# A hybrid decoder step on one core: the recurrent stage's small products placed on all four quarters of the TensorE array, and a pair's transposes put ahead of its value products

## The chip, the core and the metric

The kernel runs on one NeuronCore of one Trainium2 chip. The metric is the device time of one execution in microseconds (us), the median of several runs. The kernel before takes 2002.41 us (three runs, 1999.7 to 2004.16).

## The reference, cut to what matters

One decoder layer on 256 prompt positions and 8 sampled tokens (264 columns in all), float32: a SwiGLU feed-forward block, a mixing block (sliding-window attention beside an RWKV-7 recurrence), an output projection, a second feed-forward block, a final norm. The change touches only the recurrence, 16 heads of width 64:

```
def step(S, inp):                       # S: state [value i, key j] of a head
    sa = einsum('bhij,bhj->bhi', S, -kk_t)
    S = S * exp(lw_t) + sa[..., None] * (kk_t * a_t) + v_t[..., None] * k_t
    return S, einsum('bhij,bhj->bhi', S, r_t)
S, ys = lax.scan(step, S0, xs)          # 256 prompt steps; 1 step for each of the 8 sampled tokens
```

## The kernel before, in words

**Large products.** Every weight matrix is streamed from HBM in chunks of four 128x128 blocks (SyncE's queue, tile `raw`), split by ScalarE into a rounded part `hi` and by VectorE (or GpSimd) into a rest `lo`, and multiplied by TensorE in three fp32r products per block with 264 moving columns. These products have an accumulator tile `acc` as output (three PSUM banks). Four `hi` and four `lo` buffers let the split run ahead.

**Small work beside it.** Generators (tasks) are advanced one step after each chunk of the input projection and the output projection (`tick`). Each step issues its instructions there, and the Tile scheduler then orders each engine's instructions by its own timing estimate; every engine runs its list strictly in that order. All small products of the tasks write tiles named `m`, which share five PSUM banks (`mp()`, NM = 5): a sixth tile has to wait until the readers of the first are through.

**The recurrence** is done in chunks of 64 positions. Eight pairs of heads (`prep`, one task per pair) build the factors of the chunks; four batches of two pairs (`chain`) then solve and carry the state. A pair holds its two heads on partitions 0 to 63 and 64 to 127 (`HALF[0]`, `HALF[1]`, index h). A product with 64 contraction rows and 64 output columns occupies one quarter of the 128x128 array: its rows are the partitions of its inputs, its columns the partitions of its output. Written as (row half, column half), the kernel before uses (0,0) for h = 0 and (1,1) for h = 1. The places, with the names that the profile shows as out<-moving,stationary or with the two inputs in the other order:

- `XD,ld` in `prep`: 16 products per pair, state of a sampled token (64x64, in `ld`) by two columns of `XD`, into `dps`; ScalarE copies one column out (L488), VectorE reads the other from PSUM.
- `kr,bk`: eight 64x128 products into two banks, masked into `gm` by VectorE; then two transposes (L510), eight `uv,gm` products into `gv` (copied by L520 into `KR[:, 2]`), and four transposes (L523) copied into `BT`.
- `TN,gm` and `TT,zs` in `chain`: two groups of 16 products of 32x32 per batch, each copied out by two ScalarE copies (L596, L605) that the next group reads.
- `kr,TT`: 16 products per batch, 64 rows, 64 columns, moving 128 columns (`KR[r, 0:3:2]`: both W and UV at once), copied out by L619, L620, L621.
- `BT,W` and `gm,W`: 12 + 12 products per batch; `uv,BT` and `gm,uv`: 16 + 16 with all 128 rows and 64 columns.
- The carry loop: three steps per batch, each four products `S,PT` (or `N,PT`) and four `kr,S` (or `kr,N`), the latter added into `pY`, which ends in the tile `y` (L674).

Float32 products appear in the trace as two records each (16 products are x32); the large fp32r products and the transposes as one.

Of the kernel before, what the change touches and what calls it, by code (L numbers as in the profile page):

```python
# [10 lines left out]
ALU = mybir.AluOpType  # L11
AX = mybir.AxisListType

P = 128
NP = 256
NB = 8
# [8 lines left out]
HALF = (slice(0, 64), slice(64, 128))  # L25
# [22 lines left out]
def body(tc, I, O):  # L48
    nc = tc.nc
    V, A, G, TE, SP = nc.vector, nc.scalar, nc.gpsimd, nc.tensor, nc.sync  # L50
# [6 lines left out]
    def tt(e, out, a, b, op):  # L57
        return e.tensor_tensor(out=out, in0=a, in1=b, op=op)  # L58
# [14 lines left out]
    def mm(out, lhsT, rhs, start=True, stop=True, **k):  # L73
        TE.matmul(out, lhsT, rhs, start=start, stop=stop, **k)  # L74
# [20 lines left out]
    with ExitStack() as ctx:  # L95
# [17 lines left out]
        def mp():  # L113
            return pp.tile([P, 512], F32, tag="m", bufs=NM, name=uid("m"))
# [243 lines left out]
        def mixing_body(mx, n2, n3, XD):  # L358
# [60 lines left out]
            def prep(p, bt, k, xrr, xk, xv):  # L419
# [21 lines left out]
                W, Wi = tmp((P, 4, 65)), tmp((P, 4, 64))  # L441
# [14 lines left out]
                BK, KR = ring((P, 4, 3, 64), "bk", 2), ring((P, 3, 4, 64), "kr", NKR)  # L456
# [31 lines left out]
                A.copy(XD[:, 0, p, :], dv[:, 0])  # L488
                tt(V, dq, bps[:, T:T + 2 * NB].rearrange("p (s b) -> p s b", s=2), XD[:, 0:4:3, p, :], ALU.mult)
                tt(V, dq[:, 0], dv[:, 1], dq[:, 0], ALU.subtract)  # L490
                tt(V, XD[:, 7, p, :], dq[:, 0], dq[:, 1], ALU.add)
                yield
                gps = [mp(), mp()]
                for c in range(4):
                    for h in range(2):
                        r = HALF[h]
                        mm(gps[h][:, c * P:(c + 1) * P], BK[r, c, h:h + 2, :], KR[r, 0:2, c, :])
                for h in range(2):
# [3 lines left out]
                    for blk in range(2):  # L502
                        x = blk * 32
# [7 lines left out]
                for e in range(2):  # L511
                    for h in range(2):
                        A.copy(KR[HALF[h], 0, e:4:2, :],
                               kp[HALF[e], :256].rearrange("p (c t) -> p c t", c=2)[:, :, HALF[h]])
# [5 lines left out]
                A.copy(KR[:, 2], gv[:, :256].rearrange("p (c t) -> p c t", c=4))  # L520
                bp = mp()
                for c in range(4):
                    TE.transpose(bp[:, c * P:(c + 1) * P], BK[:, c, 0:2, :], ident)  # L523
# [3 lines left out]
                for h in range(2):  # L527
                    A.copy(BT[HALF[h], :, HALF[1]], bp[HALF[1 - h], :, HALF[1]])
                bt.BT[k] = BT
                yield  # L530
                bt.left -= 1

# [10 lines left out]
            def chain(bt):  # L543
                n = bt.n
# [13 lines left out]
                TT = ring((P, n * 4, 64), "TT", NTT)  # L558
# [11 lines left out]
                for g in range(ng):  # L570
                    d = Y[g * nr:(g + 1) * nr].rearrange("p j t -> p (j t)")
# [13 lines left out]
                yield  # L585
                ps = mp()
                for k in range(n):
                    for c in range(4):
                        for h in range(2):
                            j = k * 4 + c  # L590
                            mm(ps[h * 64 + 32:h * 64 + 64, j * 32:j * 32 + 32],
                               bt.Gm[k][h][h * 64:h * 64 + 32, c, 32:64], TN[h * 64:h * 64 + 32, j, :])
                zs = ring((P, n * 4, 32), "zs", 1)
                for h in range(2):
                    r = slice(h * 64 + 32, h * 64 + 64)
                    A.copy(zs[r], ps[r, :n * P].rearrange("p (c t) -> p c t", t=32))  # L596
                yield
                ps = mp()
                for j in range(4 * n):
                    for h in range(2):  # L600
                        r = slice(h * 64 + 32, h * 64 + 64)
                        mm(ps[h * 64:h * 64 + 32, j * 32:j * 32 + 32], zs[r, j, :], TT[r, j, 32:64])
                for h in range(2):
                    r = slice(h * 64, h * 64 + 32)
                    A.copy(TT[r, :, 32:64], ps[r, :n * P].rearrange("p (c t) -> p c t", t=32))  # L605
# [5 lines left out]
                wus = [mp() for _ in range(n)]  # L611
                for k in range(n):
                    for c in range(4):
                        for h in range(2):
                            r = HALF[h]
                            mm(wus[k][r, c * P:c * P + P], TT[r, k * 4 + c, :], bt.KR[k][r, 0:3:2, c, :])
                for k in range(n):
                    v = wus[k].rearrange("p (c t) -> p c t", c=4)
                    A.copy(W[:, k], v[:, 1:4, 0:64])  # L619
                    V.tensor_copy(uv[HALF[0], :, k, HALF[0]], v[HALF[0], :, 64:128])  # L620
                    A.copy(uv[HALF[1], :, k, HALF[1]], v[HALF[1], :, 64:128])  # L621
                yield
                pbs = [mp() for _ in range(n)]
                for k in range(n):
                    for c in range(1, 4):
                        x = (c - 1) * P
# [3 lines left out]
                        for h in range(2):  # L630
                            r = HALF[h]
                            mm(pbs[k][r, x + 64:x + P], W[r, k, c - 1, :], bt.Gm[k][h][r, c, 64:128])
                for k in range(n):
                    v = pbs[k][:, :384].rearrange("p (c t) -> p c t", c=3)
                    A.copy(PT[:, k], v[:, :, 0:64])
                    tt(V, bt.KR[k][:, 1, 1:4, :], v[:, :, 64:128], bt.KR[k][:, 1, 1:4, :], ALU.add)
# [7 lines left out]
                for k in range(n):  # L644
                    for c in range(4):
                        x = (k * 4 + c) * 64
                        for h in range(2):
                            r = HALF[h]
                            mm(pY[r, x:x + 64], uv[:, c, k, r], bt.Gm[k][h][:, c, 64:128],
                               k + c == 0, c == 0, skip_group_check=True)  # L650
                tt(V, N, pN[:, :n * 256].rearrange("p (k c t) -> p k c t", k=n, c=4),
                   bc(wc[:, bt.p0:bt.p0 + n, :].unsqueeze(3), (P, n, 4, 64)), ALU.mult)
# [2 lines left out]
                for c in range(1, 4):  # L655
                    ps = mp()
                    for k in range(n):
                        for h in range(2):
                            r = HALF[h]
                            mm(ps[r, k * 64:k * 64 + 64], PT[r, k, c - 1, :], S[r, k])  # L660
                    for k in range(n):
                        for h in range(2):
                            r = HALF[h]
                            x = (k * 4 + c) * 64
                            mm(pY[r, x:x + 64], S[r, k], bt.KR[k][r, 1, c, :], False, True, skip_group_check=True)
                    Z, Sn = ring((P, n, 64), "Z", 2), ring((P, n, 64), "S", 3)
                    for k in range(n):
                        stt(Z[:, k], S[:, k], wc[:, bt.p0 + k, c:c + 1], N[:, k, c, :], ALU.mult, ALU.add)
                    for k in range(n):
                        stt(Sn[:, k], ps[:, k * 64:k * 64 + 64], wc[:, bt.p0 + k, c:c + 1], Z[:, k], ALU.mult, ALU.add)  # L670
                    S = Sn
                    yield
                for k in range(n):
                    A.copy(Ys[k][:, :NP], pY[:, k * NP:(k + 1) * NP])  # L674
# [397 lines left out]
```

## Time and profile before

| | |
|---|---|
| median of the runs | 2002.41 us (1999.7 to 2004.16) |
| profiled execution | 2002.93 us, span in the trace 2001.1 us |
| granted TensorE clock, mean | 0.997 |
| busy: PE, DVE, ACT | 1980.3, 1304.9, 1055.0 us |
| HBM read | 347.59 MB, 179 GB/s over the span |
| stage of the recurrence and the attention | about 770 to 1160 us of the span |

The page gives each engine's busy time, the chain of work that ended last, and the costliest groups. The timeline gives instructions in order of time, like ones merged: start, time until the last of them ended, engine, line, operation, output<-inputs, shape (rows*columns of the array for PE, then moving rows x columns), and their number. PE rows overlap, since a product's stated time includes its run through the array; how long a group holds the engine is the distance from its start to the start of the next row.

### The profile page before, as it was taken

The page shows a single profiled execution, that of the slowest core. Times are in us where ns is not written, and L with a number is a line of the kernel's source. Part 1 is how long each engine was busy: PE and PEld are TensorE (multiplying, and loading weights), DVE is VectorE, ACT ScalarE, POOL GpSimd, SP SyncE. Part 2 cuts the span into 40 slices and gives each one's busy share as a digit, 9 for nine tenths or more (in the row PEclk, how much of TensorE's full clock was granted, in tenths as well). Part 3 has the DMA queues.
Part 4 walks back from the last instruction along what each step waited for, and adds up shares of the span by engine and source line. Part 5 has one row for each costly group of instructions (what it writes and reads, how often), then busy time and mean ns, then how long its engine had stood idle before and what let it go on. Part 6 is the DMA issues. An engine that isn't in the chain of part 4 may idle for free.

```text
span 2001.1 us, 45661 instructions
## 1 busy us (share of the span) xinstructions
PE 1980.3 (99%) x17116; PEld 1945.5 (97%) x17116; DVE 1304.9 (65%) x2550; ACT 1055.0 (53%) x2089; POOL 340.3 (17%) x437
## 2 busy tenths in 40 slices
PE   9999999999999999999999999999999999999998
PEld 9999999999999999998988899999999999999997
DVE  5865555655556577688768766765666666666665
ACT  5644444444444456765555655654444444444445
POOL 0401001010010122121123553120101001010012
PEclk9999999999999999999999999999999999999999
DMA  7666666665666567554555546565666666666664
GB/s 231 177 193 192 184 193 191 184 184 177 186 176 185 182 197 221 158 149 130 152 143 148 155 141 195 175 182 177 189 188 193 182 188 195 184 192 183 195 180 145
DMA packets 229230, 358.74 MB, mean 179 GB/s; under 512 B 42616, under 2 KB 84240, under 8 KB 229008
## 3 DMA queue, kind: packets, MB, share of 16 engines
q1 hardware_dynamic: 223120, 349.72, 58.4%
q10 hardware_dynamic: 5888, 6.11, 1.0%
q8 instruction: 134, 2.20, 0.5%
q14 instruction: 88, 0.72, 0.1%
HBM read 347.59 MB, written 10.22 MB: 179 GB/s over the span
## 4 chain that ended last, share of the span: by engine, by line
PE 94%; DVE 3%; DMA 2%; SPq 1%; ACT 0%; issue 0%; POOL 0%; DVEq 0%; POOLq 0%; ACTq 0%
PE acc L74 86%; PE m L74 7%; DVE lo L58 0%; DVE Xt L58 0%; DMA Xt<-sa 0%; DMA raw<-in_gu 0%; DVE st L58 0%; DMA xg<-in_xT 0%; SPq L126 0%; DVE y L58 0%; PE m L523 0%; DVE t L703 0%; ACT hi L127 0%; DMA TT<-sb 0%; SPq L555 0%
## 5 line engine op out<-in xcount | busy, mean ns | idle before, releaser
L127 ACT CAST hi<-raw 128x512 fp32r<-128x512 f32 (+2 forms) x1304 | 779.0, 602 | 822.0 <-PE acc L74 733.5
L58 DVE TENSOR_TENSOR lo<-raw,hi 128x512 fp32r<-128x512 f32 (+1 forms) x1248 | 854.0, 688 | 540.0 <-ACT hi L127 515.5
L74 PE MATMUL acc<-s,hi 128*128 128x264 f32 x5940 | 1109.7, 286 | 0.3 <-ACT hi L127 0.2
L74 PEld LDWEIGHTS acc<-s,hi 128*128 128x128 f32 x5940 | 923.8, 188 | 7.4 <-issue 2.2
L74 PE MATMUL acc<-s,lo 128*128 128x264 f32 x2970 | 848.9, 286 | 2.5 <-DVE lo L58 2.5
L74 PEld LDWEIGHTS acc<-s,lo 128*128 128x128 f32 x2970 | 558.7, 188 | 7.0 <-DVE lo L58 3.6
L74 PE MATMUL acc<-t,hi 128*128 128x264 f32 x2752 | 502.8, 284 | 0.0
L74 PEld LDWEIGHTS acc<-t,hi 128*128 128x128 f32 x2752 | 425.9, 188 | 0.0
L74 PE MATMUL acc<-t,lo 128*128 128x264 f32 x1376 | 388.5, 284 | 0.0
L58 POOL TENSOR_TENSOR t<-t,t 128x264 f32<-128x264 f32 (+1 forms) x148 | 150.8, 1019 | 1149.0 <-ACT hi L127 789.6
L74 PEld LDWEIGHTS acc<-t,lo 128*128 128x128 f32 x1376 | 258.2, 188 | 0.1
L74 PE MATMUL acc<-y,hi 128*128 128x264 f32 x648 | 123.9, 284 | 0.0
L74 PEld LDWEIGHTS acc<-y,hi 128*128 128x128 f32 x648 | 101.2, 188 | 0.2
L74 PE MATMUL acc<-y,lo 128*128 128x264 f32 x324 | 91.2, 282 | 0.0
L58 DVE TENSOR_TENSOR t<-acc,t 128x264 f32<-128x264 f32 x156 | 67.4, 432 | 36.3 <-PE acc L74 36.1
L58 POOL TENSOR_TENSOR lo<-raw,hi 128x512 fp32r<-128x512 f32 x56 | 74.5, 1333 | 58.3 <-ACT hi L127 34.0
L58 POOL TENSOR_TENSOR o<-o,o 128x264 f32<-128x264 f32 x43 | 35.9, 834 | 187.3 <-ACT o L68 183.4
L74 PE MATMUL acc<-o,hi 128*128 128x264 f32 x324 | 62.4, 282 | 0.0
L74 PEld LDWEIGHTS acc<-y,lo 128*128 128x128 f32 x324 | 60.9, 188 | 0.0
L61 DVE SCALAR_TENSOR_TENSOR s<-acc,s 128x264 f32<-128x264 f32 x96 | 40.5, 427 | 16.0 <-PE acc L74 15.5
L74 PEld LDWEIGHTS acc<-o,hi 128*128 128x128 f32 x324 | 49.9, 188 | 0.0
L74 PE MATMUL m<-s,hi 128*128 128x264 f32 x260 | 48.1, 285 | 0.0
(249 smaller groups left out, 1350.5 us busy)
## 6 DMA issues: line engine op xcount, KB each, us to landing
raw<-in_gu SPq DMA_DIRECT2D x688, 256.0 KB, 3.4
raw<-in_dn SPq DMA_DIRECT2D x224, 256.0 KB, 2.9
raw<-in_win SPq DMA_DIRECT2D x152, 256.0 KB, 3.5
raw<-in_dn SPq DMA_DIRECT2D x160, 192.0 KB, 2.7
raw<-in_wout SPq DMA_DIRECT2D x48, 256.0 KB, 3.3
raw<-in_wout SPq DMA_DIRECT2D x32, 128.0 KB, 3.1
s<-xsp SPq DMA_DIRECT2D x16, 132.0 KB, 3.7
ld<-in_sT SPq DMA_DIRECT2D x16, 128.0 KB, 3.8
```

What stands on the lines that cost most here:

```text
L58: return e.tensor_tensor(out=out, in0=a, in1=b, op=op)
L61: return V.scalar_tensor_tensor(out=out, in0=a, scalar=s, in1=b, op0=op0, op1=op1)
L74: TE.matmul(out, lhsT, rhs, start=start, stop=stop, **k)
L127: A.copy(hi[:, :w], raw[:, :w])
```

## The change

Products that stood on the two diagonal quarters are now spread over four. Where two products of one half h follow each other, every other one gets the opposite column half, `HALF[1 - h]`, so that its result stands on the wrong partitions, in a bank of its own; the copy out of PSUM reads it there and writes it to the right partitions. Such a copy handles one half at a time, so one copy of 128 partitions becomes one of 128 partitions with half the columns and two of 64 partitions. `dps` and `gv` take two banks in place of one. The 32x32 products get a second column position for the batch's second pair, and their loops run over c outside k; each group's two copies become four. The 16 products `kr,TT` with 128 moving columns become 28 products with 64 (W is not computed for the first chunk). In a pair, the four transposes into `bp` and the copies into `BT` now come before the `uv,gm` products. In the carry loop the two kinds of product alternate pair by pair. `sub(h, x)` is the 32 partitions from 64h + 32x. The diff, without the renaming of slices:

```diff
-                dps = mp()
+                dps = [mp(), mp()]
                 for i in range(NB):
                     for h in range(2):
                         r = HALF[h]
-                        mm(dps[r, 2 * i:2 * i + 2], st[i // 4][r, i % 4, :], XD[r, 6:8, p, i])
-                dv = dps[:, 0:16].rearrange("p (b s) -> p s b", s=2)
-                A.copy(XD[:, 0, p, :], dv[:, 0])
+                        x = i // 2 * 2
+                        mm(dps[i % 2][HALF[h ^ i % 2], x:x + 2], st[i // 4][r, i % 4, :], XD[r, 6:8, p, i])
+                dv = [d[:, 0:NB].rearrange("p (b s) -> p s b", s=2) for d in dps]
+                A.copy(XD[:, 0:7:6, p, 0:NB:2], dv[0])
+                for h in range(2):
+                    A.copy(XD[HALF[h], 0:7:6, p, 1:NB:2], dv[1][HALF[1 - h]])
...
-                tt(V, dq[:, 0], dv[:, 1], dq[:, 0], ALU.subtract)
+                tt(V, dq[:, 0], XD[:, 6, p, :], dq[:, 0], ALU.subtract)
...
-                gv = mp()
-                for c in range(4):
-                    for h in range(2):
-                        r, o = HALF[h], HALF[1 - h]
-                        mm(gv[r, c * 64:c * 64 + 64], bt.Gm[k][h][o, c, 0:64], bt.UV[o, c, k, r])
-                A.copy(KR[:, 2], gv[:, :256].rearrange("p (c t) -> p c t", c=4))
                 bp = mp()
...
                 bt.BT[k] = BT
+                gv = [mp(), mp()]
+                for c in range(4):
+                    for h in range(2):
+                        r, o = HALF[h], HALF[1 - h]
+                        x = c // 2 * 64
+                        mm(gv[c % 2][HALF[h ^ c % 2], x:x + 64], bt.Gm[k][h][o, c, 0:64], bt.UV[o, c, k, r])
...
-                for k in range(n):
-                    for c in range(4):
+                for c in range(4):
+                    for k in range(n):
                         for h in range(2):
                             j = k * 4 + c
-                            mm(ps[h * 64 + 32:h * 64 + 64, j * 32:j * 32 + 32],
-                               bt.Gm[k][h][h * 64:h * 64 + 32, c, 32:64], TN[h * 64:h * 64 + 32, j, :])
+                            mm(ps[sub(h, 1 - k), j * 32:j * 32 + 32],
+                               bt.Gm[k][h][sub(h, 0), c, 32:64], TN[sub(h, 0), j, :])
...
+                        for ps, a, m in (pW, 0, 0), (pU, 2, 1):
+                            for h in range(2):
+                                if a or c:
+                                    mm(ps[HALF[h ^ m], j * 64:j * 64 + 64], TT[HALF[h], j, :],
+                                       bt.KR[k][HALF[h], a, c, :])
...
-                            mm(pbs[k][r, x:x + 64], W[r, k, c - 1, :], bt.BT[k][r, c, r])
-                        for h in range(2):
-                            r = HALF[h]
-                            mm(pbs[k][r, x + 64:x + P], W[r, k, c - 1, :], bt.Gm[k][h][r, c, 64:128])
+                            mm(pP[HALF[1 - h], x:x + 64], W[r, k, c - 1, :], bt.BT[k][r, c, r])
+                        for h in range(2):
+                            r = HALF[h]
+                            mm(pG[r, x:x + 64], W[r, k, c - 1, :], bt.Gm[k][h][r, c, 64:128])
...
-                            mm(pY[r, x:x + 64], S[r, k], bt.KR[k][r, 1, c, :], False, True, skip_group_check=True)
+                            mm(pY[HALF[1 - h], x:x + 64], S[r, k], bt.KR[k][r, 1, c, :], False, True,
+                               skip_group_check=True)
...
-                    A.copy(Ys[k][:, :NP], pY[:, k * NP:(k + 1) * NP])
+                    for h in range(2):
+                        A.copy(Ys[k][HALF[h], :NP], pY[HALF[1 - h], k * NP:(k + 1) * NP])
```

What TensorE's list holds at three places. First, the products `XD,ld` of the fifth pair and what follows them; before, with the bonus product `t,C` ahead and the first batch's `TN,gm` behind (the number after an `m` tells the PSUM tile):

```order
L74 MATMUL m_12799<-t_12681,C 128x280 [waits DVE_49,PE_49,Pool_49]
L74 MATMUL m_12802<-XD,ld_12725 64x2 [waits DMAHW5_49]
L74 MATMUL m_12802<-XD,ld_12725 64x2 x7
L74 MATMUL m_12802<-XD,ld_12727 64x2 [waits DMAHW7_49]
L74 MATMUL m_12802<-XD,ld_12727 64x2 x7
L74 MATMUL m_12848<-TN_12790,gm_11263 32x32 [waits PE_49]
```

and now:

```order
L74 MATMUL m_12823<-t_12705,C 128x280 [waits DVE_49,PE_49,Pool_49]
L74 MATMUL m_12826<-XD,ld_12749 64x2 [waits DMAHW5_49]
L74 MATMUL m_12826<-XD,ld_12749 64x2
L74 MATMUL m_12827<-XD,ld_12749 64x2 [waits PE_49]
L74 MATMUL m_12827<-XD,ld_12749 64x2
L74 MATMUL m_12826<-XD,ld_12749 64x2 x2
L74 MATMUL m_12827<-XD,ld_12749 64x2 x2
L74 MATMUL m_12826<-XD,ld_12751 64x2 [waits DMAHW7_49]
L74 MATMUL m_12826<-XD,ld_12751 64x2
L74 MATMUL m_12827<-XD,ld_12751 64x2 x2
L74 MATMUL m_12826<-XD,ld_12751 64x2 x2
L74 MATMUL m_12827<-XD,ld_12751 64x2 x2
```

The place in the list is the same; two tiles (12826 on the diagonal quarters, 12827 on the other two) alternate every two products.

Second, `kr,TT` of the first batch; before, 16 products with 128 moving columns:

```order
L74 MATMUL m_12958<-kr_11127,TT_11726 64x128 [waits DMAHW1_49,DVE_49,Activation_49]
L74 MATMUL m_12959<-kr_11492,TT_11726 64x128 [waits PE_49]
L74 MATMUL m_12958<-kr_11127,TT_11726 64x128 [waits DMAHW4_49,Activation_49]
L74 MATMUL m_12958<-kr_11127,TT_11726 64x128 x6
L74 MATMUL m_12959<-kr_11492,TT_11726 64x128 x7
```

and now 28 products with 64, the first half of which is:

```order
L74 MATMUL m_12990<-kr_11127,TT_11738 64x64 [waits DMAHW7_49,DVE_49,Activation_49]
L74 MATMUL m_12990<-kr_11127,TT_11738 64x64 [waits DMAHW1_49,Activation_49]
L74 MATMUL m_12989<-kr_11127,TT_11738 64x64 [waits PE_49]
L74 MATMUL m_12989<-kr_11127,TT_11738 64x64
L74 MATMUL m_12990<-kr_11127,TT_11738 64x64 x2
L74 MATMUL m_12989<-kr_11127,TT_11738 64x64 x2
L74 MATMUL m_12990<-kr_11127,TT_11738 64x64 x2
L74 MATMUL m_12989<-kr_11127,TT_11738 64x64 x2
L74 MATMUL m_12990<-kr_11127,TT_11738 64x64 x2
```

Each pair of heads now sends eight products to the off-diagonal quarters (12990) and six to the diagonal ones (12989).

Third, the end of ScalarE's work for the same links: the copies out of `XD,ld`, `TN,gm` and `TT,zs`; before:

```order
L488 COPY XD<-m_12802 128x8 [waits PE_49]
L596 COPY zs_12865<-m_12848 32x256 [waits PE_49]
L596 COPY zs_12865<-m_12848 32x256
L127 CAST hi_13258<-raw_13257 128x512 [waits DMAHW7_49,DVE_49,PE_49]
L68 ACTIVATE t_12828<-pj_10571,vec 128x256 [waits DVE_49]
L605 COPY TT_11726<-m_12906 32x8x32 [waits PE_49]
L605 COPY TT_11726<-m_12906 32x8x32
```

and now:

```order
L489 COPY XD<-m_12826 128x2x4 [waits PE_49,Pool_49]
L491 COPY XD<-m_12827 64x2x4 [waits PE_49]
L491 COPY XD<-m_12827 64x2x4
L610 COPY zs_12892<-m_12875 32x128 [waits PE_49]
L610 COPY zs_12892<-m_12875 32x128 x3
L127 CAST hi_13249<-raw_13248 128x512 [waits DMAHW6_49,PE_49,Activation_49]
L621 COPY TT_11738<-m_12935 32x4x32 [waits PE_49]
L621 COPY TT_11738<-m_12935 32x4x32 x3
```

Five copies became eleven; the split of the next weight chunk (`hi`) still stands between the two groups. Over the whole list ScalarE has 225 rows of copies where it had 193 (a row can stand for several), VectorE has 28 where it had 32. In two of the eight pairs (the sixth and the eighth) the list has runs of five to seven `XD,ld` products into one tile; in the fifth and the seventh the `uv,gm` products stand as four into one tile, eleven large products, and four into the other; and in the first two batches six `BT,W` products of the first pair stand ahead of its six `gm,W`.

More of the change, by code (lines that the diff above doesn't have):

```diff
@@ L529, in prep @@
                 bt.BT[k] = BT
+                gv = [mp(), mp()]
[4 more added lines that the diff above has]
+                        mm(gv[c % 2][HALF[h ^ c % 2], x:x + 64], bt.Gm[k][h][o, c, 0:64], bt.UV[o, c, k, r])
+                gv = [g[:, :P].rearrange("p (c t) -> p c t", c=2) for g in gv]
+                A.copy(KR[:, 2, 0:4:2], gv[0])
+                for h in range(2):
+                    A.copy(KR[HALF[h], 2, 1:4:2], gv[1][HALF[1 - h]])
                 yield
@@ L610, in chain @@
                 N = ring((P, n, 4, 64), "N", 1)
-                wus = [mp() for _ in range(n)]
+                pW, pU = mp(), mp()
                 for k in range(n):
                     for c in range(4):
+                        j = k * 4 + c
+                        for ps, a, m in (pW, 0, 0), (pU, 2, 1):
+                            for h in range(2):
+                                if a or c:
+                                    mm(ps[HALF[h ^ m], j * 64:j * 64 + 64], TT[HALF[h], j, :],
+                                       bt.KR[k][HALF[h], a, c, :])
@@ new lines, in chain @@
+                pW, pU = (ps.rearrange("p (k c t) -> p k c t", k=n, c=4) for ps in (pW, pU))
+                A.copy(W, pW[:, :, 1:4, :])
+                V.tensor_copy(uv[HALF[0], :, :, HALF[0]].rearrange("p c k t -> p k c t"), pU[HALF[1]])
+                A.copy(uv[HALF[1], :, :, HALF[1]].rearrange("p c k t -> p k c t"), pU[HALF[0]])
+                yield
+                pP, pG = mp(), mp()
+                for k in range(n):
+                    for c in range(1, 4):
+                        x = (k * 3 + c - 1) * 64
@@ L633, in chain @@
+                pP, pG = (ps[:, :n * 192].rearrange("p (k c t) -> p k c t", k=n, c=3) for ps in (pP, pG))
+                for h in range(2):
+                    A.copy(PT[HALF[h]], pP[HALF[1 - h]])
                 for k in range(n):
-                    v = pbs[k][:, :384].rearrange("p (c t) -> p c t", c=3)
-                    A.copy(PT[:, k], v[:, :, 0:64])
-                    tt(V, bt.KR[k][:, 1, 1:4, :], v[:, :, 64:128], bt.KR[k][:, 1, 1:4, :], ALU.add)
+                    tt(V, bt.KR[k][:, 1, 1:4, :], pG[:, k], bt.KR[k][:, 1, 1:4, :], ALU.add)
@@ L673, in chain @@
                 for k in range(n):
-                    A.copy(Ys[k][:, :NP], pY[:, k * NP:(k + 1) * NP])
+                    for h in range(2):
+                        A.copy(Ys[k][HALF[h], :NP], pY[HALF[1 - h], k * NP:(k + 1) * NP])
                     A.copy(Ys[k][:, NP:T], XD[:, 7, bt.p0 + k, :])
```

37 lines of the change are left out of this document (15 added, 22 removed).

## Prediction, made before the changed kernel was run

> **What bounds the kernel.** I read the page first: busy shares and the chain that ended last.
>
> ```profile
> span 2001.1 us, 45661 instructions
> PE 1980.3 (99%) x17116; PEld 1945.5 (97%) x17116; DVE 1304.9 (65%) x2550; ACT 1055.0 (53%) x2089; POOL 340.3 (17%) x437
> PE 94%; DVE 3%; DMA 2%; SPq 1%; ACT 0%; issue 0%; POOL 0%; DVEq 0%; POOLq 0%; ACTq 0%
> ```
>
> TensorE (PE) is on the path for 94% of the span. A busy PE can still be waiting inside, so I took stages next (us; busy time and count of PE, its weight loads PEld, DVE, ACT, POOL; clock; DMA share; GB/s) and then PE's waits (total us, times, longest).
>
> ```profile
> 100.00:690.00 590.00, 590.00 (x4856) 590.00 (x4855) 339.70 (x577) 277.49 (x486) 60.76 (x56) 1.00 0.62 186
> 900.00:1000.00 100.00, 95.87 (x1165) 88.96 (x1165) 81.75 (x237) 59.66 (x146) 17.52 (x41) 1.00 0.53 142
> 770.00:1160.00 390.00, 380.54 (x3984) 351.10 (x3984) 293.67 (x824) 252.24 (x625) 106.95 (x190) 1.00 0.54 152
> ...
> PE m L74 <- ACT t L68: 3.3, 2, 2.2
> PE acc L74 <- DVE lo L58: 2.5, 4, 0.8
> PE m L74 <- DVE N L58: 1.1, 1, 1.1
> ```
>
> From 100 to 690 us the large products come every 590/4856 = 0.1215 us, without a gap. In the recurrent stage, 770 to 1160, PE is idle for 390 − 380.5 = 9.5 us. So a us less of PE work there should be nearly a us less of time, as long as VectorE (75% busy there, 82% from 900 to 1000) and ScalarE (65%) keep up.
>
> **What the small products cost now.** Timeline around the fifth pair and the first batch (start, us, what):
>
> ```profile
> 910.88 1.10 PE L74 MATMUL m<-XD,ld 64*64 64x2 f32 x32
> 911.90 0.69 PE L74 MATMUL m<-TN,gm 32*32 32x32 f32 x32
> 912.52 1.16 PE L74 MATMUL m<-kr,bk 64*128 64x128 f32 x16
> ...
> 919.12 2.02 PE L74 MATMUL m<-kr,TT 64*64 64x128 f32 x32
> 921.07 0.44 PE L510 MATMUL m<-C,kr 128*128 128x128 f32 x2
> 921.44 0.68 PE L74 MATMUL m<-uv,gm 64*64 64x64 f32 x16
> 922.05 0.66 PE L523 MATMUL m<-C,bk 128*128 128x128 f32 x4
> ...
> 924.23 0.33 PE L74 MATMUL m<-BT,W 64*64 64x64 f32 x4
> 924.39 0.28 PE L74 MATMUL m<-gm,W 64*64 64x64 f32 x4
> ...
> 925.56 0.28 PE L74 MATMUL m<-gm,W 64*64 64x64 f32 x4
> 925.77 1.15 PE L74 MATMUL m<-uv,BT 128*64 128x64 f32 x32
> ...
> 933.44 0.45 PE L74 MATMUL m<-S,PT 64*64 64x64 f32 x8
> 933.72 0.40 PE L74 MATMUL m<-kr,S 64*64 64x64 f32 x8
> 934.05 0.39 PE L74 MATMUL acc<-s,lo 128*128 128x264 f32 x1
> ```
>
> From 924.39 to 925.56 there are ten such rows of four records: 1.17/40 = 29.2 ns a record with two quarters in use, so each quarter takes 58.5 ns a record. `XD,ld` moves only two columns and still takes 32 × 29.2 = 0.93 of its 1.02 us: the quarter's weight load sets that, not the columns. The rest, 0.09 to 0.14 us a group, is the turn from one array shape to the next and stays.
>
> **Do four quarters run at once?** No row before has that. The nearest (a short window each, then two whole groups):
>
> ```profile
> 912.52 0.38 PE L74 MATMUL m<-kr,bk 64*128 64x128 f32 x2
> ...
> 1095.86 0.32 PE L74 MATMUL m<-uv,bk 128*32 128x128 f32 x4
> ...
> 1096.83 0.28 PE L74 MATMUL m<-s,bk 128*32 128x1 f32 x16
> 1097.04 0.43 PE L74 MATMUL m<-t,s 128*64 128x256 f32 x1
> ```
>
> The first window (20 ns wide) holds the starts of both row halves, over the same columns into two banks. The second (25 ns) holds the starts of four column quarters that share all their rows. In the third, 16 records with their own weights fit in 0.21 us, 13 ns each with the turn included. So row halves overlap, column quarters overlap, and starts can follow each other within 14.6 ns. The bounds per record are 14.6 (four at once) and 29.2 ns (no gain); I take 14.6, since the rows of four column quarters are nearest.
>
> [...]
>
> **The sum, term by term** (two-at-once time halved, turns left alone):
> - `XD,ld`, eight pairs: 0.93 to 0.47 us, 8 × 0.47 = 3.7.
> - `uv,gm`, eight pairs: 16 × 29.2 = 0.47 of 0.61 us, halved, 8 × 0.23 = 1.9.
> - `TN,gm` and `TT,zs`: 0.62 us from the row to the next, 0.12 of it the turn; 8 groups × 0.25 = 2.0.
> - `kr,TT`: 1.95 us, 0.15 of it the turn. Now the fullest quarters take eight products, 16 records × 58.5 = 0.94 us; 4 × (1.80 − 0.94) = 3.4.
> - `BT,W` and `gm,W`: 48 records, 1.54 us with the turn; 4 × 0.70 = 2.8.
> - carry loop: 16 records a step, 12 steps × 0.23 = 2.8.
>
> That makes 16.6 us. `uv,BT`, `gm,uv` and `kr,bk` keep their shape: nothing. From it go the places where the list of the changed kernel doesn't alternate: two pairs of `XD,ld` (−0.8), two batches' first half of `BT,W` (−0.7), two pairs of `uv,gm` cut in two by large products (−0.5). The two lists hold 185 and 186 changes of array shape, so turns cost −0.1. Left: **14.5 us of PE time**. The transposes moved ahead of `uv,gm` are the same transposes between the same two turns: nothing.
>
> **The copies.** ScalarE durations (min/median/max ns):
>
> ```profile
> L488 ACT COPY XD<-m x8: 166/166/166, 811.0 to 1028.2; 128x8 f32<-128x8 f32 x8
> L520 ACT COPY kr<-m x8: 372/373/375, 816.1 to 1037.1; 128x256 f32<-128x256 f32 x8
> L596 ACT COPY zs<-m x8: 363/364/367, 912.6 to 1124.9; 32x256 f32<-32x256 f32 x8
> L513 ACT COPY kr<-m x32: 254/260/265, 813.8 to 1034.1; 64x128 f32<-64x128 f32 x32
> L674 ACT COPY y<-m x8: 349/369/379, 937.3 to 1147.8; 128x256 f32<-128x256 f32 x8
> ```
>
> A copy costs by its columns, hardly by its partitions: 0.17 us for 8, 0.26 for 128, 0.37 for 256. `XD`: two more, +0.33, eight times 2.7. `gv`: three of 0.26 for one of 0.37, 8 × 0.41 = 3.3. `zs` and `TT`: four of 0.26 for two of 0.36, 8 × 0.31 = 2.5. `y`: two more of 0.37 in four batches, 3.0. `W`, UV and `PT` trade fewer copies for wider ones, about even. Together +11.5 us of ScalarE, which is idle for 390 − 252 = 138 us of the stage: hidden as work. As latency, `zs` and `TT` stand right ahead of products that read them; between `TN,gm` and `TT,zs` the list has `kr,bk` (912.52 to 913.62, 1.1 us) and six large products (0.7 us), which cover four copies (1.04 us) unless a 0.6 us split of a chunk goes first. If the cover is gone, 0.31 us × 8 = 2.5. I charge these in full, and 1.0 more for PE's waits on `lo`, since PE reaches its large products 0.25 to 0.7 us earlier after each burst while VectorE does not: the four waits of 2.5 us in all would grow by 0.25 each. Give-back 3.5, between nothing and all of 14.5.
>
> **Sum.** 2002.93 (profiled execution; span 2001.1) − 14.5 + 3.5 = 1991.9. The median of the runs is 0.5 below the profiled execution: **1991.4 us**.
>
> **Rivals.**
> - **VectorE takes over** between 900 and 1100 us: the 82% becomes 87% if 6 us leave that stretch, and its list runs in order, with the solve's small steps between the `lo`. Each of some 36 bursts (8 pairs with two each, 4 batches with five) then gives back 0.25 us: 9. 2002.4 − 14.5 + 9 = 1997. For it: VectorE's share there, and that `lo` is already waited for. Against: the rows above have PE waiting for VectorE for 2.5 and 1.1 us in all.
> - **The quarters take turns** (the change doesn't do what it says): 29.2 ns stays. `kr,TT` becomes 56 × 29.2 = 1.64 for 1.80, −0.6 over four batches; the copies' latency adds 1: 2003. Against: the column-quarter rows. [...]
> - **PSUM banks** (slower): `XD,ld` and `uv,gm` claim one more of the five `m` banks each, 16 claims. A claim can last until VectorE has read the bonus tile behind the copies:
>
> ```profile
> 912.02 0.17 ACT L488 COPY XD<-m 128x8 f32<-128x8 f32 x1 [1.70 <-PE m L74]
> ...
> 913.82 0.17 DVE L58 TENSOR_TENSOR t<-m,XD 128x16 f32<-128x16 f32 x1
> ```
>
>  `XD,ld` ended at 911.9 and that read at 914.0, 2.1 us later. If PE, which runs in order, sat out 1.4 us per claim with the large products queued behind it: 16 × 1.4 = 22, 2010 us. It cancels the gain at 14.5/16 = 0.9 us a claim and shows as slower from 1.2. For it: five banks are just what one pair needs from the bonus product to `kr,bk` (1 + 2 + 2), and `TN,gm` makes it six. Against: the list puts large products in where it expects such a wait, and PE's waits of today are for values (`t`, `lo`, `N`).
>
> **How the numbers follow.** Forecast 1991.4, own range 1986 to 1996: 0.60. More than that (waits of today gone too): 0.04. VectorE: 0.14, three quarters of it still faster by over 0.2%. Turns: 0.09, of it 0.07 no change, the rest on both sides. Banks: 0.13. A difference under 0.2% (4 us) is about what a measurement of this kernel can't tell from no change. Faster 0.60 + 0.04 + 0.11 + 0.01 = 0.76; same 0.03 + 0.07 = 0.10; slower 0.13 + 0.01 = 0.14. The range takes in the forecast, VectorE and the turns: 1985 to 2004; the banks and the tail below are left out, under 0.2.
>
> **What would show it.** `XD,ld` x32 from its start to the next row about 0.55 us (1.02 now), `uv,gm` x16 0.38, `TN,gm` 0.37, `kr,TT` x56 1.1, `BT,W` with `gm,W` 0.85: then four run at once. If these distances stay, it was turns. If they shrink and the span doesn't, PE's waits tell which rival: on `lo` (VectorE), on `zs` or `TT` (copies), or idle time ahead of `kr,bk`, `uv,gm` with ScalarE or VectorE as releaser (banks). The forecast is wrong if small products shrink by under 10 us or PE's idle time in the stage grows by over 8.

## The result, and the profile after

**No change that can be measured.** The changed kernel takes 2003.59 us (median of 14 runs, 2001.57 to 2005.91), the kernel before 2001.71 beside it (14 runs, 1999.70 to 2006.54): ratio 1.0006, 95% interval 0.9998 to 1.0014 (all ratios here are of the means, so they differ a little from those of the medians). 1991.4 was predicted, 12 us less. The execution profiled after is the fastest of its 14 (2001.57), that of before (2002.93) lies 1.2 above its median; so the two profiles differ by -1.4 us where the medians differ by +1.9. What follows compares the profiles and says so.

The page after: span, busy engines, the shares of the chain of work that ended last; then the stages (columns as before), of which the middle row is the recurrent stage.

```profile
span 1999.8 us, 45897 instructions
PE 1969.5 (98%) x17212; PEld 1933.6 (97%) x17212; DVE 1301.4 (65%) x2546; ACT 1065.4 (53%) x2137; POOL 343.1 (17%) x437
PE 91%; DVE 4%; DMA 2%; ACT 1%; issue 1%; SPq 1%; POOL 0%; ACTq 0%; DVEq 0%; POOLq 0%
```

```profile
100.00:690.00 590.00, 590.00 (x4856) 590.00 (x4855) 340.14 (x577) 277.28 (x486) 60.52 (x56) 1.00 0.61 186
770.00:1160.00 390.00, 372.06 (x4093) 341.19 (x4093) 290.65 (x820) 264.43 (x676) 109.73 (x193) 0.99 0.53 152
900.00:1000.00 100.00, 91.49 (x1202) 83.95 (x1203) 80.52 (x231) 61.30 (x159) 17.97 (x43) 0.97 0.50 138
```

PE is busy 10.8 us less (1980.3 to 1969.5), so the work did shrink. But span minus busy, PE's idle time, went from 20.8 to 30.3 us, and PE's share of the chain from 94 to 91%. The timeline around the fifth pair and the first batch shows the smaller products:

```profile
910.79 0.64 PE L74 MATMUL m<-XD,ld 64*64 64x2 f32 x32
911.36 0.45 PE L74 MATMUL m<-TN,gm 32*32 32x32 f32 x32
911.75 1.49 PE L74 MATMUL m<-kr,bk 64*128 64x128 f32 x16
...
917.12 1.15 PE L74 MATMUL m<-kr,TT 64*64 64x64 f32 x56
918.20 0.44 PE L513 MATMUL m<-C,kr 128*128 128x128 f32 x2
...
919.01 0.45 PE L74 MATMUL m<-uv,gm 64*64 64x64 f32 x8
...
922.12 0.45 PE L74 MATMUL m<-uv,gm 64*64 64x64 f32 x8 [1.13 <-ACT W L637]
...
923.09 0.56 PE L74 MATMUL m<-BT,W 64*64 64x64 f32 x12
925.62 0.59 PE L74 MATMUL m<-gm,W 64*64 64x64 f32 x6 [1.97 <-ACT uv L639]
```

From its start to the next row `XD,ld` takes 0.57 us (1.02 before; 0.55 foretold), `TN,gm` 0.39 (0.62; 0.37), `kr,TT` 1.08 (1.95; 1.1). The starts of four records of `kr,TT` lie 6 to 7 ns apart, then in most of the group comes a step of 38: 58 ns for four, where two quarters took 58 for two. So four quarters do run at once. The two waits in the last rows are new. ScalarE's rows for the same time show where they come from:

```profile
921.05 0.51 ACT L68 ACTIVATE t<-pj,vec 128x256 f32<-128x256 f32 x1 [4.30 <-DVE pj L58]
921.59 0.48 ACT L637 COPY W<-m 128x384 f32<-128x384 f32 x1
...
924.99 0.58 ACT L639 COPY uv<-m 64x512 f32<-64x512 f32 x1 [1.18 <-DVE uv L638]
```

The last record of `kr,TT` ends at 918.3, but the copy of its result into `W` starts at 921.59: in ScalarE's list it stands behind an operation that waits 4.30 us for VectorE's `pj`. The copy itself takes 0.48 us. `uv,gm` starts when it is done (922.12 after 922.07), though it doesn't read `W`, so it waits for the bank that the copy empties. The copy into `uv` waits 1.18 us for VectorE's copy of the other half, which starts at 924.26, between two steps of the solve. PE's waits in the stage, after (total us, times, longest):

```profile
PE acc L74 <- DVE lo L58: 4.6, 4, 1.8
PE m L74 <- ACT W L637: 3.2, 2, 2.1
PE m L74 <- DVE st L58: 3.1, 2, 2.4
PE m L74 <- ACT t L68: 3.1, 3, 1.7
PE m L74 <- ACT uv L639: 2.2, 2, 2.0
```

Before, `lo` stood for 2.5 us, `W` for 0.3, `st` and `N` together for 1.3, `uv` for nothing; the two rows of before that the prediction doesn't show are:

```profile
PE m L74 <- ACT W L619: 0.3, 1, 0.3
PE m L74 <- DVE st L58: 0.2, 1, 0.2
```

Where the waits on `W` and `uv` of the first batch lie, the granted clock falls too (the last three figures of a row: clock, DMA share, GB/s):

```profile
920.00:925.00 5.00, 2.53 (x32) 1.94 (x30) 4.66 (x18) 2.67 (x9) 1.52 (x4) 0.93 0.27 85
925.00:930.00 5.00, 4.38 (x90) 4.26 (x92) 4.49 (x21) 3.09 (x8) 0.00 (x0) 0.50 0.19 44
930.00:935.00 5.00, 5.00 (x59) 4.61 (x56) 2.97 (x12) 3.05 (x5) 0.32 (x3) 0.89 0.15 31
```

In the trace's record of the clock this is one stretch of 6.8 us at half rate in the stage, which costs up to 3.4 us; before there is one of 3.4 us, which costs up to 1.7. That gives a ledger for the two profiles: products -12.5 (busy time without the clock's part), clock +1.7, idle +9.5, in all -1.3 us of span.

### The profile page after: what moved, and what is told of

Its sections match the earlier page's. It is cut to its first block, busy times and chain, and to the rows that moved or that the text cites. A ratio compares the mean times of both kernels' runs of the same rounds, so it can differ in the third digit from the quotient of the medians.

```text
span 1999.8 us, 45897 instructions
## 1 busy us (share of the span) xinstructions
PE 1969.5 (98%) x17212; PEld 1933.6 (97%) x17212; DVE 1301.4 (65%) x2546; ACT 1065.4 (53%) x2137; POOL 343.1 (17%) x437
## 4 chain that ended last, share of the span: by engine, by line
PE 91%; DVE 4%; DMA 2%; ACT 1%; issue 1%; SPq 1%; POOL 0%; ACTq 0%; DVEq 0%; POOLq 0%
PE acc L74 84%; PE m L74 6%; DVE lo L58 1%; DMA raw<-in_gu 1%; DVE st L58 1%; DVE Xt L58 1%; DMA raw<-in_win 0%; ACT t L68 0%; ACT hi L127 0%; DMA sb<-Xt 0%; DMA TT<-sb 0%; DVE y L58 0%; SPq L562 0%; DMA Xt<-sa 0%; SPq L563 0%
## 5 line engine op out<-in xcount | busy, mean ns | idle before, releaser
L58 DVE TENSOR_TENSOR t<-acc,t 128x264 f32<-128x264 f32 x156 | 67.4, 432 | 35.9 <-PE acc L74 35.7
```

## The experiments

In the tables, "idle" is the span minus PE's busy time, "clock" half the length of the half-rate stretches between 800 and 1200 us, and "products" is busy minus clock, all of the profiled execution. "Clock" is an upper bound, so "products" is good to a few us only: for the same products the kernel before shows 1974.2 to 1980.4 in five lists (1971.0 with pauses of seven). Ratios are against the kernel before, run on the same chip; differences of medians between rows are often between chips or times at which the kernel before took 2001.7 to 2003.1.

### Which waits: links or VectorE?

Theory A: the gain goes at the links of the chain (waits on `W`, `uv`, `N`, behind wider copies and shared banks). Theory B: VectorE's list sets the pace. Theory C: each edit makes the scheduler write another list, and that moves the waits about.

**Half of the change each.** First the preparation alone, then the chain alone (each the hunks of the diff that belong to it).

> Only the preparation of a pair is changed (state products XD,ld and value products uv,gm on four quarters with their copies, transposes ahead); the chain is the kernel before's. In the two traces these products went from 8.2 to 5.3 us (XD,ld) and from 6.1 to 5.1 us (uv,gm), 3.9 us in all. Theory A (links: the gain is given back in the chain, where PE waits for the wider merged copies W and uv and for the banks that they hold): the waits of the chain are not there, so about -3.5 us, ratio 0.998. Theory B (VectorE's list between 850 and 1072 us is the limit, so that any PE time saved there comes back as waits on it): 0, ratio 1.000. Theory C (a changed list reshuffles the scheduler's order and moves waits about by several us, whatever is saved): anything from -4 to +4, and the halves do not add up to the whole.

> Only the chain is changed (TN,gm, TT,zs, kr,TT, BT,W with gm,W, carry loop on four quarters, with their copies); the preparation of a pair is the kernel before's. Products saved in the two traces: TN,gm 0.95, TT,zs 0.8, kr,TT 3.3, loop 2.4, about 7.5 us without the stalls of BT,W. Theory A: PE's waits on W and uv (5.4 us in the changed kernel, 0.3 before) are all here, so -1 to -2 us, or a bit slower, ratio 0.999 to 1.001. Theory B: 0, ratio 1.000, and the waits that grow are those on lo, st and N and not on W and uv. Theory C: anything from -6 to +4.

Measured 2014.39 us for the preparation (ratio 1.0058, 1.0044 to 1.0071) and 2004.45 for the chain (1.0013, 1.0003 to 1.0023). The halves cost +12.5 and +2.6, the whole +1.9: they don't add up. A and B had nothing to make the preparation slower by 12 us. C has, but its own range, 4 us either way, was missed by far.

**Without the solve.**

```diff
-                    t = ring((ng * nr, m, w), "st", 2)
-                    shp = (ng * nr, m, w)
-                    tt(V, t, bc(X[:, s:s + 1, s + 1:], shp), bc(Y[:, :m, s:s + 1], shp), ALU.mult)
-                    tt(V, Y[:, :m, s + 1:], Y[:, :m, s + 1:], t, ALU.add)
```

> The kernel before without the 30 steps of the triangular solve on VectorE (240 instructions of about 0.21 us, 50 us between 850 and 1072 us); the solve is left out of the computation, all else stays. VectorE's share from 900 to 1000 us falls from 82 to about 60%. Its own waits on lo, N and st are 2.5 + 1.1 + 0.2 us. All theories: -2 to -4 us, 1998 to 2000. It is the base for the next kernel.

> The changed kernel without the 30 steps of the triangular solve on VectorE (left out of the computation, as in the kernel before it). Against the kernel before without the solve: theory B: the whole saving of 11 to 13 us of products appears, about 10 us faster than its base, near 1988. Theory A: the waits on lo and st that grew by 2.1 and 1.8 us go, those on W and uv (5.4 us) stay, so 4 to 6 us faster than its base. Theory C: within 3 us of its base.

Measured 1996.13 (before, ratio 0.9963, 0.9949 to 0.9978) and 1996.67 (changed, 0.9973, 0.9963 to 0.9983). Both lie 5 to 6 us below the kernel before, and the change is still worth nothing: between the two profiles products fall by 13.5 us, idle time grows by 7.5 and the clock's part by 5.1. Theory C's forecast, within 3 us of each other, held; 10 (B) and 4 to 6 us faster (A) missed. PE's waits of 0.5 us and more in the stage, before and then changed, both without the solve:

```profile
PE m L74 <- DVE N L58: 3.5, 1, 3.5
PE acc L74 <- POOL s L58: 0.9, 1, 0.9
```

```profile
PE acc L74 <- DVE lo L58: 3.1, 1, 3.1
PE m L74 <- ACT W L633: 2.9, 1, 2.9
PE m L74 <- ACT XD L489: 2.6, 2, 2.0
PE acc L74 <- POOL s L58: 1.8, 1, 1.8
PE m L74 <- DVE y L61: 0.9, 1, 0.9
PE m L74 <- DVE t L787: 0.5, 2, 0.3
```

VectorE is now busy for 67 to 68% of 900 to 1000 us, so B falls in the sense that VectorE has too much to do. The wait on `lo` comes at 852 us while VectorE itself stands idle, its list held up by a step that waits for a DMA of the solve's result:

```profile
854.80 0.43 DVE L587 STREAM_TRANSPOSE TN<-TT 32x256 f32<-32x256 f32 x1 [5.51 <-DMA TT<-sb]
855.17 0.64 DVE L58 TENSOR_TENSOR lo<-raw,hi 128x512 fp32r<-128x512 f32 x1
```

So an engine with time to spare makes PE wait, because in its list `lo` stands behind that step.

**More time at the links.**

```diff
                 A.copy(uv[HALF[1], :, :, HALF[1]].rearrange("p c k t -> p k c t"), pU[HALF[0]])
+                yield
                 yield
...
                    bc(wc[:, bt.p0:bt.p0 + n, :].unsqueeze(3), (P, n, 4, 64)), ALU.mult)
+                yield
                 yield
```

> The changed kernel with one more chunk of large products between kr,TT with its copies and BT,W, and one more between gm,uv with N and the first step of the carry loop; nothing is computed otherwise. Theory A (PE waits at the links for W, uv and N: 3.2 + 2.2 + 3.1 us): these waits go, 5 to 8 us faster than the changed kernel, 1996 to 1999. Theory B: the time comes back as waits on lo, 2003. Theory C: a new list, -5 to +5 with waits at other places than now.

Measured 2007.80 (1.0028, 1.0017 to 1.0039), 4 us slower than the changed kernel, with these waits still there:

```profile
PE acc L74 <- DVE lo L58: 4.2, 4, 1.4
PE m L74 <- DVE Xt L58: 2.8, 1, 2.8
PE m L74 <- ACT W L637: 2.3, 2, 1.1
PE m L74 <- DVE y L58: 2.2, 2, 1.6
PE m L74 <- ACT uv L639: 2.0, 1, 2.0
```

This speaks against A: a chunk more between copy and reader took little off `W` (3.2 to 2.3) and `uv` (2.2 to 2.0), and new waits came. It is no clean test, since this edit too makes a new list.

### The same work in other lists

**Products on two quarters, copies and banks as changed.** At six places, such as

```diff
-                                    mm(ps[HALF[h ^ m], j * 64:j * 64 + 64], TT[HALF[h], j, :],
+                                    mm(ps[HALF[h], j * 64:j * 64 + 64], TT[HALF[h], j, :],
```

> The changed kernel with its copies, banks and order of loops, but with the 64-row products back on the two diagonal quarters (their results then stand where the turned copies don't look, so values are wrong; only the 32x32 products stay spread). What four quarters are worth under the changed list: kr,TT, XD,ld, uv,gm and the loop lose about 10 us of PE time again. If PE's work counts one to one (A, C: the loss sits in copies and list), it is 9 to 11 us slower than the changed kernel, near 2013. If the other engines set the pace in this stage (B), the waits shrink as PE gets slower and it is 0 to 3 us slower, 2004 to 2007.

**Longer pauses**, nine chunks and then seven (`DWAIT`), in the kernel before and in the changed one.

```diff
-DWAIT = (8, 8, 8, 8)
+DWAIT = (9, 9, 9, 9)
```

> The kernel before with its pauses around the solve nine chunks long in place of eight (DWAIT). Same work, another list. Theories A and B: within 2 us of the kernel before, since no link that PE waits on gets shorter. Theory C (the list of the kernel before is an unusually good one, and any new list costs several us of waits and of small groups cut in two): 4 to 10 us slower than the kernel before, 2006 to 2012.

> The changed kernel with the same pauses of nine chunks. Theories A and B: within 2 us of the changed kernel, so still 1 to 3 us slower than its partner with nine. Theory C: another draw of the list, 1998 to 2008, and 5 to 12 us faster than the kernel before with nine, since the saving in products is there in both lists.

> The kernel before with pauses of seven chunks around the solve in place of eight. Same work, another list. Nine chunks gave 2011.7. Theory C (the list of the kernel before is a good draw; another list of the same work costs several us): 4 to 12 us slower than the kernel before, 2006 to 2014. Theory F (eight is simply the right length for the DMAs that the pauses cover, and the time rises on both sides of it by what the DMAs are then waited for): also slower, but with the growth in waits for tiles that the solve's DMAs fill (Xt, TN) and the same for the changed kernel.

> The changed kernel with pauses of seven chunks. Nine gave 2004.2, eight 2003.6. Theory C: another draw, 1998 to 2010, and on the whole faster than its partner of the kernel before by some 5 to 10 us. Theory F: slower than with eight by what its partner is, 2007 to 2013, and no faster than that.

**The moved transposes**: only this move in the kernel before, and all but this move.

> The kernel before with only the four transposes into bp and the copies into BT put ahead of the products uv,gm (which stay on two quarters, in one bank). Same work, another list. Theory C: 3 to 12 us slower than the kernel before. If the transposes' place does what the words of the change may suggest and costs nothing: within 2 us of it.

> The changed kernel with the products uv,gm back ahead of the four transposes; everything else as changed. Theory C: another draw, 1998 to 2010, 5 to 10 us faster than the mean of the other lists of the kernel before. If the moved transposes are what spoils the change: 5 us or more faster than the changed kernel.

**Two more neutral edits**, each in the kernel before, in the changed one on the diagonal quarters, and in the changed one: P, nine chunks for the first batch alone; Q, one more chunk in `prep`.

```diff
-DWAIT = (8, 8, 8, 8)
+DWAIT = (9, 8, 8, 8)
```

```diff
-PW = (2, 1, 3, 2, 2)
+PW = (3, 1, 3, 2, 2)
```

> The kernel before with the first batch's pauses nine chunks long, the others eight. Same work, another list. The kernel before has 20.8 us of PE idle time; two other lists of the same work had 25.5 and 26.9. Theory C (its list is an unusually good one): idle time 24 to 28 us, 4 to 10 us slower than the kernel before. If the copies and banks of the change alone are what costs idle time: 20 to 22 us of idle time, within 2 us of the kernel before.

> The changed kernel with the first batch's pauses nine chunks long and the 64-row products on the diagonal quarters (values wrong, as in the earlier one of this kind). Its idle time against that of its partner of the kernel before is what the copies and banks cost: theory C 0 to 2 us, so 0 to 2 us slower than that partner; if copies and banks cost the idle time of the change, 5 to 7 us slower.

> The changed kernel with the first batch's pauses nine chunks long. Against its partner on the diagonal quarters: 10 to 12 us less product time, of which 3 to 4 come back as idle time and up to 3 as half clock (theory C): 4 to 7 us faster than it, and 4 to 8 faster than its partner of the kernel before. If the other engines set the pace: no faster than either.

> The kernel before with one more chunk of pause in the preparation of a pair (PW, first number 3 in place of 2). Same work, another list. Theory C: 4 to 10 us slower than the kernel before, idle time 24 to 28 us. If copies and banks cost the idle time of the change: within 2 us of the kernel before.

> The changed kernel with one more chunk of pause in the preparation of a pair and the 64-row products on the diagonal quarters (values wrong, as in the two earlier ones of this kind). Its partner of the kernel before measured 2009.8. Theory C: within 5 us of it either way (another draw, copies and banks worth about nothing). If copies and banks cost idle time: 5 to 7 us slower.

> The changed kernel with one more chunk of pause in the preparation of a pair. Theory C: 4 to 8 us faster than its partner on the diagonal quarters, and 3 to 12 us faster than its partner of the kernel before (2009.8), so 1998 to 2006. If the other engines set the pace: no faster than either.

| products as in | list | median us | ratio (95%) | products | idle | clock |
|---|---|---|---|---|---|---|
| before | its own | 2001.71 | | 1978.6 | 20.8 | 1.7 |
| before | pauses nine | 2011.72 | 1.0047 (1.0031-1.0062) | 1980.4 | 26.9 | 3.4 |
| before | transposes moved | 2011.04 | 1.0048 (1.0031-1.0065) | 1978.1 | 25.5 | 5.1 |
| before | P | 2011.58 | 1.0040 (1.0025-1.0055) | 1975.9 | 27.0 | 6.8 |
| before | Q | 2009.83 | 1.0033 (1.0022-1.0045) | 1974.2 | 29.2 | 6.8 |
| diagonal | as changed | 2008.70 | 1.0034 (1.0022-1.0047) | 1977.9 | 27.3 | 1.7 |
| diagonal | P | 2006.53 | 1.0017 (1.0008-1.0027) | 1975.7 | 24.2 | 5.1 |
| diagonal | Q | 2009.02 | 1.0028 (1.0016-1.0040) | 1975.4 | 26.1 | 5.1 |
| changed | its own | 2003.59 | 1.0006 (0.9998-1.0014) | 1966.1 | 30.3 | 3.4 |
| changed | pauses nine | 2004.24 | 1.0007 (0.9996-1.0017) | 1960.5 | 33.3 | 6.8 |
| changed | transposes not moved | 2002.54 | 1.0012 (1.0000-1.0024) | 1967.9 | 28.3 | 5.1 |
| changed | P | 1999.21 | 0.9980 (0.9971-0.9990) | 1964.4 | 30.2 | 1.7 |
| changed | Q | 2009.38 | 1.0027 (1.0012-1.0041) | 1965.2 | 35.7 | 3.4 |
| before | pauses seven | 2023.31 | 1.0105 (1.0090-1.0120) | 1971.0 | 36.8 | 13.7 |
| changed | pauses seven | 2029.67 | 1.0138 (1.0123-1.0153) | 1958.8 | 43.9 | 25.6 |

Three things are to be read from it.

*The list of the kernel before is out of the ordinary.* Four edits that leave its products alone each make it 7 to 9 us slower, and its idle time goes from 20.8 to between 25.5 and 29.2. One of them, the move of the transposes, is part of the change, and of the half that cost 12.5 us; yet in the changed kernel, taking the move back makes no difference that can be measured (ratios 1.0006 and 1.0012). Whether the kernel before has its good list by chance, or because its pauses were chosen to suit it, no run here shows. Where the time goes differs from list to list. PE's longest waits with the transposes moved, and then with nine chunks:

```profile
PE acc L74 <- DVE lo L58: 3.8, 4, 1.3
PE m L74 <- ACT uv L621: 2.0, 1, 2.0
PE m L74 <- ACT t L68: 1.9, 3, 1.0
PE acc L74 <- POOL s L58: 1.8, 1, 1.8
```

```profile
PE acc L74 <- DVE lo L58: 10.3, 7, 4.3
PE m L74 <- DVE uv L620: 1.2, 2, 0.7
```

The first of these waits 2.0 us on `uv` with the narrow copies of the kernel before: that wait needs no part of the change but the order.

*The copies and banks cost nothing that shows.* On the diagonal quarters, with all of the change's copies, the idle time is 27.3, 24.2 and 26.1, no more than in the four other lists of the kernel before. Under P this kernel is 5 us faster than its partner, under Q 1 us. Both expectations for the diagonal kernel under P, no gain (C) and 5 to 7 us slower (copies and banks), missed; so did my 9 to 11 us between diagonal and changed. This was seen with the slower PE. In the change's own list the waits on `W` and `uv` come to 5.4 us with four quarters and 1.9 with two, under P to 1.8 and 2.4.

*What the four quarters are worth depends on the list.* Diagonal to changed, with the change's own pauses, under P and under Q: products -11.8, -11.3 and -10.2; idle +3.0, +6.0 and +9.6; median -5.1, -7.3 and +0.4 us, which is 43%, 65% and nothing of what the products save. The two of a pair don't run quite the same list either. Counting the large products ahead of each record of a small one, 477 of the 2716 records stand at another place in the first pair, 531 under P and 1868 under Q; the four neutral edits move 1465 to 1996 of the 2620 in the kernel before. So the first two pairs compare nearly the same list, and there about a half comes through; under Q two different lists are compared, and the quarters can't be told from the list. Against the kernel before under the same edit, the changed one stands at -7.5 (nine), -7.4 (transposes moved), -12.4 (P) and -0.4 (Q), 7 us in the mean; but it stands at +1.9 and about +1 against the list that the kernel before came with. Seven chunks are another matter: the kernel before loses 22 us there, and the changed one 26, more than theory C gave them (2006 to 2014 and 1998 to 2010). VectorE's longest waits for a DMA in the stage, in the kernel before with eight and then with seven chunks, show that the pause no longer covers the transfers:

```profile
DVE TN L584 <- DMA TT<-sb: 8.1, 4, 3.6
```

```profile
DVE TN L584 <- DMA TT<-sb: 21.5, 4, 7.7
```

Under Q theory C missed (4 to 8 us faster than the diagonal partner, 1998 to 2006), and the reading that the other engines set the pace came true: no faster than either. Why Q's list is bad for the changed kernel and P's is good stays open.

Of the versions that leave nothing out, the changed kernel under P is the one that beats both kernels: 1999.21 us, 0.10 to 0.29% below the kernel before. Its lines of span and busy time:

```profile
span 1996.3 us, 45897 instructions
PE 1966.1 (98%) x17212; PEld 1931.8 (97%) x17212; DVE 1300.7 (65%) x2546; ACT 1065.9 (53%) x2137; POOL 341.2 (17%) x437
```

Since it was the best of seven lists of the changed kernel (six in the table, one with more time at the links), part of that is the choice.

## Why the prediction was wrong

- **Four quarters at once: right.** 58 ns for four records, 14.6 each, as taken from the column quarters. The starts within a four lie 6 to 7 ns apart, with two quarters on each half of the rows. The rival of taking turns falls; no row of before spoke for it, and its 0.09 was my estimate.
- **The terms: right.** Summed over the distances between starts, `XD,ld` went from 8.2 to 5.3 us in all (2.9 measured; 3.7 less 0.8 foretold), `uv,gm` from 6.1 to 5.1 (1.0; 1.4), `TN,gm` with `TT,zs` 1.75 (2.0), `kr,TT` from 7.6 to 4.3 (3.3; 3.4), the carry loop 2.4 (2.8). `BT,W` with `gm,W` is hidden by a wait in the changed kernel; without the solve, where no wait falls into it, it saved 2.1 (2.8 less 0.7). Together 13.5 for 14.5, and 12.5 by the ledger. That the weight load sets the pace of `XD,ld` was my reading: before, a quarter's loads start about 58 ns apart whether 2 columns move (`XD,ld`) or 64 (`BT,W`), and no run changes the loads alone.
- **The copies: right.** ScalarE's busy time rose by 10.4 us (11.5 foretold), hidden as work, and the diagonal kernels show no price in idle time. The 2.5 us charged for their latency didn't come: the changed kernel has no wait on `zs` or `TT`.
- **The give-back of 3.5 us: here it failed.** Idle time and clock took 9.5 + 1.7 = 11.2. The step rested on the sentence that a us less of PE work in the stage is nearly a us less of time, and on the waits of the kernel before as they stood, with 0.25 us more on four of them. Two things were missing. The change makes a new list: with the products still on two quarters, idle time already goes from 20.8 to 27.3 us, as in the other lists of the kernel before (25.5 to 29.2). And a faster PE meets the events of the other engines earlier: in the two pairs with nearly the same list, idle time grows by another 3.0 and 6.0. So of the 9.5 us some 6.5 go with the new list (with its copies and banks) and 3.0 with the four quarters; since even these lists differ in places, that split is an estimate. I had compared the two lists for changes of array shape, 185 and 186, but took the waits of the old list as if they came along. The waits that came were on copies held up in the lists of ScalarE and VectorE (the rows at 921 and 925 us), which no term of the sum had.
- **The rivals.** VectorE as the bound falls, since the give-back stays without the solve (7.5 + 5.1 us). The banks: the waits ahead of `uv,gm` and `gm,W` did show, 1.1 and 2.0 us in the first batch, far from 16 claims of 1.4. Under P the wait on `uv` is 0.2 us and the idle time as long (30.2), so they aren't the whole; under Q (2.0) and with nine chunks (1.7) such a wait is there, and the share of the banks stays open. The mark for "wrong" was well put: PE's idle time in the stage grew by 8.5 us (9.5 to 17.9), over 8.
- **The range: luck.** 2003.59 lies within 1985 to 2004, but only at the end that was put there for quarters taking turns, which they don't. No change had been given 0.10, most of it for that reason.

## What to carry to other kernels

Where a scheduler or pools write the engines' lists, price a change against several lists of the same work (here a neutral edit of a pause moved the time by 7 to 9 us, as much as the change was worth in the mean), and not against the one list that the kernel came with. Where PE is 96 to 98% busy in a stage of many small links, a saving in its work need not come through in full: here about a half did in two lists, and nothing in a third. After such a change, try the neutral edits again before judging it.

## What was not expected of the hardware

In the trace's record of the clock the granted clock falls to 0.50 in stretches of 3.41, 6.83, 10.24 or 13.65 us: one of 3.41 in the stage before (from 1030.96 us), one of 6.83 in the changed kernel (from 924.30), seven in the changed kernel with pauses of seven chunks, where they cost up to 25.6 us (mean granted clock of that execution 0.985; 0.997 before). The products slow down with it: before, the large ones start 0.22 us apart inside the stretch (1033.28 to 1033.50) and 0.12 after it (1034.50 to 1034.62). In the traces of all twenty kernels there are 51 stretches between 800 and 1200 us, and each begins during an idle time of PE, 0.3 to 4.9 us long, or within 2.5 us of its end: before, 0.96 us after one of 1.48 us; in the changed kernel, during the one of 1.97 us that ends at 925.62. The reverse doesn't hold: of 50 idle times of 1.9 us or more, after 12 no such stretch begins within 2.5 us, two of them in the changed kernel (2.12 us on `W` and 2.35 on `st`, after 1052 us). So in these traces a wait of 2 us is often followed by a stretch that costs up to another 1.7 or 3.4 us (half of 3.41 or 6.83, an estimate). That the waits cause the stretches was not tried by itself.
